# Feed-forward: both halves of a wide product's bank added in one VectorE operation of 512 columns

## The chip, the cores and the metric

One core of a Trainium2 chip runs the whole kernel. The metric is the device time of one execution in microseconds (us), the median over several runs; lower is better.

## The reference, cut to what matters

A trunk of two layers on a 512 x 1024 activation in float32: a pooling mixer in the first layer, chunked attention in the second, and after each a gated feed-forward block, which is what the change touches:

```python
def conv_ffn(h, w_gate, w_val, conv_w, conv_b, w_out):
    """out = (silu(causal_dwconv3(h W_gate)) * (h W_val)) W_out"""
    S = h.shape[1]
    a = h @ w_gate
    ap = jnp.pad(a, ((0, 0), (CONV_W - 1, 0), (0, 0)))
    a = ap[:, 0:S] * conv_w[0] + ap[:, 1:S + 1] * conv_w[1] + ap[:, 2:S + 2] * conv_w[2] + conv_b
    return (jax.nn.silu(a) * (h @ w_val)) @ w_out
# D_MODEL = 1024, SEQ = 512, D_FF = 2816, DEPTH = 2
x = x + conv_ffn(rmsnorm(x, ffn_norm[i]), ffn_w_gate[i], ffn_w_val[i], ffn_conv_w[i], ffn_conv_b[i], ffn_w_out[i])
```

## The kernel before

Activations lie with channels on the 128 partitions and the 512 frames along the columns. The hidden width of 2816 is cut into 22 blocks of 128, numbered f. Float32 precision comes from splitting each operand into a high part and a low part in a reduced format; a product is then high x high + high x low + low x high. ScalarE (ACT) makes the high part with a copy, VectorE (DVE) the low part with a subtraction (line 98 and line 99, in `split`).

Blocks 5 to 21 use Strassen's scheme (Winograd's form): gate and value of one block together take seven products of half the size (256 frames) instead of eight, and VectorE combines them. In blocks 8 to 21, `f in WIDE`, a product is "wide": one matmul of 512 columns multiplies the high part of the weights by the high and the low part of the activations side by side, so that the results land in the two halves of one PSUM bank, `o[:, 0]` and `o[:, 1]`; a matmul of 256 columns adds the low part of the weights into the first half. A wide product is therefore finished only when the two halves of its bank have been added. With 14 wide blocks in each of two layers there are 28.

A wide block f runs through these steps, one per `yield` of `strassen`:

1. product b11 into bank m; ACT copies both halves into the tile `a`
2. product b21 into a bank of its own, b (`side`)
3. product t2 on top of b11 in bank m; ACT copies both halves into the tile `val` (v in the profile)
4. product t3 into bank t (again `side`)
5. product t1 on top in bank m; the result, and t3 from bank t, go to the second half of `val`
6. product b22 on top in bank m, which makes the second half of `a`
7. product t4 on top of t3 in bank t, which makes the first half of `val`; then `hidden` does the convolution on `a`, the activation, the multiplication by `val` and the split of the result into the slot of block f

So b22 cannot start before ACT has copied t1 out of bank m, and t4 cannot start before VectorE has read t3 out of bank t. The weights of the products are split as g1 (from the gate weights), g2 (from the sum tile sa), g3 (from sb) and g4 (second half of the value weights); all four bear the names g_f_h and g_f_l. The sums sa and sb are VectorE additions of the raw weights gv. The high part of g3 sits in a tile with a single buffer, so ACT can write g3 of block f only after b22 of block f-1 has read its own.

Steps 6 and 7 of a block run between the first steps of the next one, and matmuls of the output product of the group of blocks before (`out`, on weights ow, added into X) are put in between. PE's sequence is written out by hand this way (`manual_schedule`); the sequences of ACT and VectorE are made by a list scheduler from priorities and its own cost estimates, so an edit of one instruction can move others. `tc.high_priority()` raises the priority of what it encloses. Scratch tiles of 512 columns come from tag g with six buffers.

Of the kernel before, what the change touches and what calls it, by code (L numbers as in the profile page):

```python
# [19 lines left out]
AF = mybir.ActivationFunctionType  # L20
# [20 lines left out]
HALF = S // 2  # L41
# [27 lines left out]
def trunk(ctx: ExitStack, tc: tile.TileContext, xt, xT, cols, band, edge, poolw, gv, wout, wqk, wv, wo, rel, out):  # L69
    nc = tc.nc  # L70
# [14 lines left out]
    def psum(tag, name, bufs=2):  # L85
        return ps.tile([P, S], F32, name=name, tag=tag, bufs=bufs)
# [3 lines left out]
    def g_tile(name):  # L90
        return tmp.tile([P, S], F32, name=name, tag="g", bufs=6)

    def split(raw, hi, lo, eng=None, eng_hi=None):

        if eng_hi:
            eng_hi.tensor_copy(hi, raw)
        else:
            nc.scalar.activation(hi, raw, AF.Copy)  # L98
        return (eng or nc.vector).tensor_sub(lo, raw, hi.bitcast(F32))  # L99
# [17 lines left out]
    def mm3(o, sh, sl, mh, ml, first, last, **how):  # L117

        yield nc.tensor.matmul(o, sh, mh, start=first, stop=False, **how)  # L119
        yield nc.tensor.matmul(o, sh, ml, start=False, stop=False, **how)  # L120
        yield nc.tensor.matmul(o, sl, mh, start=False, stop=last, **how)  # L121

    def run(steps):
        step = None
        for step in steps:
            pass
        return step
# [249 lines left out]
    def ffn(l, first, pool, acc, summed=None):  # L377
# [7 lines left out]
        def raw_tile(name, src, n=1024, own=False):  # L385
            raw = pool.tile([P, GM * P], F32, name=f"{name}_r", tag="or") if own else wp.tile([P, 1024], F32, name=f"{name}_r", tag="wr")
            nc.sync.dma_start(raw[:, :n], src)
            return raw
# [4 lines left out]
        def sum_tile(name):  # L393
            return pool.tile([P, 1024], F32R, name=name, tag="as", bufs=2).bitcast(F32)

        def parts(raw, n, name, out_=False, later=False):

            if out_:
                hi, lo = (out_tile(f"{name}_{c}", c) for c in "hl")
            elif next(ring) == "w":  # L400
                hi, lo = (wp.tile([P, 1024], F32R, name=f"{name}_{c}", tag=f"w{c}", bufs=2) for c in "hl")
            else:
                hi, lo = (pool.tile([P, 1024], F32R, name=f"{name}_{c}", tag=f"b{c}", bufs=1) for c in "hl")
            if later:
                nc.scalar.activation(hi[:, :n], raw[:, :n], AF.Copy)
                return hi, lo, lambda: nc.vector.tensor_sub(lo[:, :n], raw[:, :n], hi[:, :n].bitcast(F32))
            split(raw[:, :n], hi[:, :n], lo[:, :n])
            return hi, lo
# [4 lines left out]
        def hidden(f, a, finish):  # L413

            cw = [col[:, C_CW[l] + 4 * f + j:C_CW[l] + 4 * f + j + 1] for j in range(4)]
            c = g_tile(f"c{f}")
            nc.scalar.activation(c, a, AF.Identity, scale=cw[2], bias=cw[3])  # L417
            for j in range(1, 3):
                nc.vector.scalar_tensor_tensor(c[:, j:], a[:, :S - j], cw[2 - j], c[:, j:], op0=OP.mult, op1=OP.add)  # L419
            silu = nc.scalar.activation(c, c, AF.Silu)  # L420
            if l == 0 and f == NF - 1:
                with tc.issue_after(silu.ins):
                    nc.scalar.preload_act_table_set("natural_log_exp_and_others")
            finish(c)
            split(c, *slot[f])
# [152 lines left out]
        def strassen(f):  # L578

            g, v = (raw_tile(f"gv{l}_{f}_{i}", gv[l, f, i]) for i in range(2))  # L580
            sa, sb = (sum_tile(f"s{x}{f}") for x in "ab")
            a11, a12, a21, a22, s2, s3, s1, s4 = (x[:, z * S:(z + 1) * S] for x in (g, v, sa, sb) for z in range(2))
            nc.vector.tensor_add(s1, a21, a22)
            nc.vector.tensor_sub(s2, s1, a11)
            nc.vector.tensor_sub(s3, a11, a21)
            nc.vector.tensor_sub(s4, a12, s2)
            wide = f in WIDE

            def bank(tag, name):
                return psum(tag, f"st{l}_{f}_{name}", 4 if tag == "S" else 2).rearrange("p (c n) -> p c n", c=2)  # L590

            def product(o, hl, z, name, first):


                hi, lo = hl
                cs = [slice((4 * z + i) * P, (4 * z + i + 1) * P) for i in range(4)]
                how = {"skip_group_check": not first}
                if not wide:
                    for i, c in enumerate(cs):
                        run(mm3(o[:, 0], hi[:, c], lo[:, c], B[i, name][:, 0], B[i, name][:, 1], first and i == 0, i == 3, **how))  # L600
                    return
                for i, c in enumerate(cs):
                    nc.tensor.matmul(o, hi[:, c], B[i, name], start=first and i == 0, stop=False, **how)  # L603
                for i, c in enumerate(cs):
                    nc.tensor.matmul(o[:, 0], lo[:, c], B[i, name][:, 0], start=False, stop=i == 3, **how)  # L605

            def add(x, o):
                for c in range(2 if wide else 1):
                    nc.vector.tensor_add(x, x, o[:, c])  # L609

            def copy(x, rest=None):

                if wide and rest is None:
                    nc.scalar.activation(x, main.rearrange("p c n -> p (c n)"), AF.Copy)
                    nc.vector.tensor_add(x[:, :HALF], x[:, :HALF], x[:, HALF:])
                else:
                    x = x[:, HALF:] if rest is not None else x[:, :HALF]
                    nc.scalar.activation(x, main[:, 0], AF.Copy)  # L618
                    if wide:
                        if rest is not main:  # L620
                            nc.scalar.activation(rest, main[:, 1], AF.Copy)  # L621
                        nc.vector.tensor_add(x, x, main[:, 1] if rest is main else rest)

            a = pool.tile([P, S], F32, name=f"a{f}", tag="a", bufs=2)
            main, side = bank("S", "m"), bank("P", "b")
            w = parts(g, 1024, f"g1_{f}")
            product(main, w, 0, "b11", True)
            copy(a)
            yield
            product(side, w, 1, "b21", True)  # L630
            add(a[:, :HALF], side)
            yield
            val = g_tile(f"v{f}")
            w = parts(sa, 1024, f"g2_{f}")
            product(main, w, 0, "t2", False)
            copy(val)
            yield
            side = bank("S", "t")
            product(side, w, 1, "t3", True)
            yield  # L640
            w = parts(sb, 1024, f"g3_{f}")
            last = [tmp.tile([P, S], F32R, name=f"g4_{f}_{c}", tag="g", bufs=6) for c in "hl"]
            split(a22, *last)
            product(main, w, 0, "t1", False)
            with tc.high_priority():
                copy(val, a[:, HALF:])
                add(val[:, HALF:], side)
            yield
            product(main, w, 1, "b22", False)
            copy(a, main)  # L650
            yield
            product(side, last, 0, "t4", False)
            add(val[:, :HALF], side)
            hidden(f, a, lambda c: nc.vector.tensor_mul(c, val, c))
            yield

# [15 lines left out]
        with tc.manual_schedule(engines={mybir.EngineType.PE}):  # L672
            h, seed, known, made = early()
            queue, left, n = [], 0, 0
# [309 lines left out]
    with tc.tile_pool(name="ba", bufs=1) as big:  # L984
        rest = attention()
# [55 lines left out]
```

## Time and profile before

| | |
|---|---|
| median of 3 runs | 976.81 us (975.59 to 977.13) |
| the profiled execution | 976.21 us |
| its span, first to last instruction | 974.4 us |
| busy: PE matmul / weight load | 964.4 / 818.9 us |
| busy: VectorE / ScalarE / GpSimd | 810.5 / 578.8 / 103.2 us |
| mean granted TensorE clock | 0.999 |

A timeline row reads: start in us from the span's start, duration in us, engine, line, operation, out<-in by the program's names, shapes, count, and in brackets the idle time of the engine before it with what ended it. PEld is TensorE's weight load, which overlaps the matmuls. In the profile, names leave out buffer and block numbers: `st_m`, `st_b` and `st_t` are the banks m, b and t, v is `val`, c is the tile in which `hidden` works, out is a bank of the output product, `one`, u0h and the like are slots of finished hidden blocks. Instructions of one engine overlap: the next starts a little before the one before has ended.

### The profile page before, as it was taken

Reading aid. Unit: us, or ns where it says so; the run is one execution under the profiler, and the core shown is the slowest. Engines: PE = TensorE matmul, PEld = TensorE weight load, DVE = VectorE, ACT = ScalarE, POOL = GpSimd, SP = SyncE. Lnnn points to the kernel's source line nnn. Section 1 sums busy time; section 2 is a strip of 40 time slices with the busy share of each in tenths; the row PEclk is TensorE's granted clock in tenths of the full one; section 3 lists DMA queues with packets and bytes.
Section 4 is the critical chain, followed back from the end, with each engine's and each line's share of the span. In section 5 each row is a group of like instructions: output and inputs, shape, how many; then the busy total and the mean of one; then the engine's idle time right before and its main releaser. Section 6 shows DMA issues by size and latency. Waiting matters only on the chain.

```text
span 974.4 us, 14095 instructions
## 1 busy us (share of the span) xinstructions
PE 964.4 (99%) x5038; PEld 818.9 (84%) x5038; DVE 810.5 (83%) x1508; ACT 578.8 (59%) x1018; POOL 103.2 (11%) x90
## 2 busy tenths in 40 slices
PE   9999999999999999999999999999999999999998
PEld 8788988888888888888888787888998888888886
DVE  8999989999999854442777888999999999999953
ACT  7665565555556444344898988646555555555521
POOL 2300000000000013203534532000000000000000
PEclk9999999999999999999999999999999999999999
DMA  8222233232332234232343341332323323233223
GB/s 341 72 96 92 92 114 112 81 126 91 114 111 70 71 84 150 87 117 99 109 117 108 96 118 54 100 108 79 114 92 121 114 90 119 86 109 119 73 61 112
DMA packets 37430, 102.85 MB, mean 106 GB/s; under 512 B 4432, under 2 KB 7904, under 8 KB 37360
## 3 DMA queue, kind: packets, MB, share of 16 engines
q1 hardware_dynamic: 37296, 101.90, 33.1%
q8 instruction: 40, 0.66, 0.3%
q14 instruction: 30, 0.25, 0.1%
q0 software_dynamic: 32, 0.04, 0.0%
q10 hardware_dynamic: 32, 0.00, 0.0%
HBM read 95.60 MB, written 2.14 MB: 100 GB/s over the span
## 4 chain that ended last, share of the span: by engine, by line
PE 85%; DVE 10%; ACT 2%; DMA 1%; issue 1%; DVEq 0%; ACTq 0%
PE st_m L603 9%; PE out L119 8%; PE out L120 8%; PE out L121 8%; PE st_t L603 5%; PE st_m L605 5%; PE gv L120 3%; PE qk L120 3%; PE qk L119 3%; PE qk L121 3%; PE gv L119 3%; PE gv L121 3%; PE st_t L605 2%; PE st_b L603 2%; DVE g_l L99 2%; PE tp L872 2%
## 5 line engine op out<-in xcount | busy, mean ns | idle before, releaser
L120 PE MATMUL out<-one,ow_h 128*128 128x512 f32 x224 | 87.9, 392 | 0.0
L119 PE MATMUL out<-one,ow_h 128*128 128x512 f32 x224 | 87.8, 392 | 0.0
L121 PE MATMUL out<-one,ow_l 128*128 128x512 f32 x224 | 87.8, 392 | 0.0
L98 ACT ACTIVATE ow_h<-wo_r 128x640 fp32r<-128x640 f32 (+1 forms) x64 | 50.5, 789 | 55.3 <-PE out L120 46.2
L668 DVE TENSOR_TENSOR X<-out,X 128x512 f32<-128x512 f32 (+1 forms) x65 | 43.9, 677 | 35.9 <-PE out L121 35.9
L603 PE MATMUL st_m<-two,g_h 128*128 128x512 f32 x224 | 70.0, 394 | 0.2
L603 PE MATMUL st_m<-h,g_h 128*128 128x512 f32 x224 | 69.0, 389 | 0.0
L98 ACT ACTIVATE g_h<-gv_r 128x512 fp32r<-128x512 f32 (+1 forms) x68 | 57.3, 842 | 17.7 <-PE st_b L603 12.3
L99 DVE TENSOR_TENSOR g_l<-gv_r,g_h 128x512 fp32r<-128x512 f32 (+1 forms) x68 | 64.5, 949 | 0.2
L99 DVE TENSOR_TENSOR ow_l<-wo_r,ow_h 128x640 fp32r<-128x640 f32 (+1 forms) x64 | 56.4, 882 | 2.5 <-ACT ow_h L98 2.5
L419 DVE SCALAR_TENSOR_TENSOR c<-a,col,c 128x511 f32<-128x511 f32 (+1 forms) x76 | 56.2, 742 | 1.8 <-ACT c L417 1.8
L121 PE MATMUL qk<-wqk_h,two 128*128 128x512 f32 x128 | 51.4, 402 | 0.0
L119 PE MATMUL qk<-wqk_h,two 128*128 128x512 f32 x128 | 50.9, 409 | 0.0
L120 PE MATMUL qk<-wqk_l,two 128*128 128x512 f32 x128 | 50.8, 397 | 0.0
L609 DVE TENSOR_TENSOR v<-v,st_t 128x256 f32<-128x256 f32 x120 | 49.4, 412 | 1.0 <-ACT v L618 0.6
L603 PEld LDWEIGHTS st_m<-two,g_h 128*128 128x128 f32 x224 | 41.6, 188 | 10.3 <-ACT a L621 1.1
L603 PEld LDWEIGHTS st_m<-h,g_h 128*128 128x128 f32 x224 | 42.1, 188 | 9.6
L605 PEld LDWEIGHTS st_m<-two,g_l 128*128 128x128 f32 x224 | 42.0, 188 | 8.8
L98 ACT ACTIVATE g_h<-sb 128x1024 fp32r<-128x1024 f32 x34 | 36.0, 1059 | 20.2 <-PE st_m L603 17.5
L121 PEld LDWEIGHTS out<-one,ow_l 128*128 128x128 f32 x224 | 42.3, 189 | 6.4
L119 PEld LDWEIGHTS out<-one,ow_h 128*128 128x128 f32 x224 | 42.3, 189 | 6.1
L120 PEld LDWEIGHTS out<-one,ow_h 128*128 128x128 f32 x224 | 42.4, 189 | 5.3
(365 smaller groups left out, 2925.3 us busy)
## 6 DMA issues: line engine op xcount, KB each, us to landing
gv_r<-gv SPq DMA_DIRECT2D x86, 512.0 KB, 3.6
wo_r<-wout SPq DMA_DIRECT2D x32, 384.0 KB, 3.4
wo_r<-wout SPq DMA_DIRECT2D x32, 320.0 KB, 2.9
wqk_r<-wqk SPq DMA_DIRECT2D x16, 512.0 KB, 3.4
wv_r<-wv SPq DMA_DIRECT2D x8, 512.0 KB, 3.4
wo_r<-wo SPq DMA_DIRECT2D x8, 512.0 KB, 3.5
xt<-xt SPq DMA_DIRECT2D x4, 512.0 KB, 5.5
X<-xT SPq DMA_DIRECT2D x8, 256.0 KB, 7.3
```

The source lines that it names most:

```text
L98: nc.scalar.activation(hi, raw, AF.Copy)
L99: return (eng or nc.vector).tensor_sub(lo, raw, hi.bitcast(F32))
L119: yield nc.tensor.matmul(o, sh, mh, start=first, stop=False, **how)
L120: yield nc.tensor.matmul(o, sh, ml, start=False, stop=False, **how)
L121: yield nc.tensor.matmul(o, sl, mh, start=False, stop=last, **how)
L419: nc.vector.scalar_tensor_tensor(c[:, j:], a[:, :S - j], cw[2 - j], c[:, j:], op0=OP.mult, op1=OP.add)
L603: nc.tensor.matmul(o, hi[:, c], B[i, name], start=first and i == 0, stop=False, **how)
L605: nc.tensor.matmul(o[:, 0], lo[:, c], B[i, name][:, 0], start=False, stop=i == 3, **how)
L609: nc.vector.tensor_add(x, x, o[:, c])
L668: nc.vector.tensor_add(X[d][:, fs], o[:, fs], X[d][:, fs])
L872: nc.tensor.transpose(tp[:, j * P:(j + 1) * P], s_[:, j * P:(j + 1) * P], ident)
```

## The change

For a wide block the change adds both halves of a bank to a tile of 512 columns in one VectorE operation, and folds the two halves of that tile together afterwards (`fold`), where before each half of the bank was added to 256 columns on its own. This is done for b21 into `a` and for t3 into a new scratch tile `both_` (w in the profile, from tag g). ACT copies t1 with one operation of 512 columns into `both_`, where it made two copies of 256, into `val` and into the second half of `a`. For b22 and t4 the additions stay as they were. In the code of b11 the fold moves behind the addition of b21. Per wide block VectorE then has two additions of 512 columns and six of 256 instead of ten of 256, and ACT one copy of 512 instead of two of 256.

```diff
-            def add(x, o):
-                for c in range(2 if wide else 1):
-                    nc.vector.tensor_add(x, x, o[:, c])
-            def copy(x, rest=None):
...
+            def flat(o):
+                return o.rearrange("p c n -> p (c n)")
+            def fold(out, x):
+                nc.vector.tensor_add(out, x[:, :HALF], x[:, HALF:])
...
             product(main, w, 0, "b11", True)
-            copy(a)
+            if wide:
+                nc.scalar.activation(a, flat(main), AF.Copy)
...
             product(side, w, 1, "b21", True)
-            add(a[:, :HALF], side)
+            if wide:
+                nc.vector.tensor_add(a, a, flat(side))
+                fold(a[:, :HALF], a)
...
             product(main, w, 0, "t2", False)
-            copy(val)
+            if wide:
+                nc.scalar.activation(val, flat(main), AF.Copy)
+                fold(val[:, :HALF], val)
...
             product(main, w, 0, "t1", False)
             with tc.high_priority():
-                copy(val, a[:, HALF:])
-                add(val[:, HALF:], side)
+                if wide:
+                    both_ = g_tile(f"w{f}")
+                    nc.scalar.activation(both_, flat(main), AF.Copy)
+                    nc.vector.tensor_add(both_, both_, flat(side))
...
+            if wide:
+                fold(val[:, HALF:], both_)
             yield
             product(main, w, 1, "b22", False)
-            copy(a, main)
+            nc.scalar.activation(a[:, HALF:], main[:, 0], AF.Copy)
+            if wide:
+                nc.vector.tensor_add(a[:, HALF:], a[:, HALF:], main[:, 1])
             yield
             product(side, last, 0, "t4", False)
-            add(val[:, :HALF], side)
+            for c in range(2 if wide else 1):
+                nc.vector.tensor_add(val[:, :HALF], val[:, :HALF], side[:, c])
```

PE's sequence stays the same instruction for instruction. VectorE and ScalarE get new ones. Three places follow, in rows of line, operation, out<-in, shape; the long numbers in the names only tell buffers apart and differ between the two kernels.

VectorE in the first layer, from the first combination of t1 and t3 of block 10 (v_1715 is its `val`, a_1640 its `a`; a_1786 is `a` of block 11), before:

```order
L622 TENSOR_TENSOR v_1715<-v_1715,a_1640 128x256
L654 TENSOR_TENSOR c_1704<-v_1577,c_1704 128x512
L615 TENSOR_TENSOR a_1786<-a_1786 128x256
L583 TENSOR_TENSOR sb_1914<-gv_12_1_r 128x512
L609 TENSOR_TENSOR v_1715<-v_1715,st_10_t 128x256
L99 TENSOR_TENSOR g_11_l<-sb_1781,g_11_h 128x1024
L622 TENSOR_TENSOR a_1640<-a_1640,st_10_m 128x256
L99 TENSOR_TENSOR one_94<-c_1704,one_86 128x512
L609 TENSOR_TENSOR v_1715<-v_1715,st_10_t 128x256
L609 TENSOR_TENSOR a_1786<-a_1786,st_11_b 128x256
```

and now:

```order
L649 TENSOR_TENSOR w_1755<-w_1755,st_10_t 128x512
L664 TENSOR_TENSOR c_1699<-v_1574,c_1699 128x512
L583 TENSOR_TENSOR sb_1906<-gv_12_1_r 128x512
L611 TENSOR_TENSOR v_1710<-w_1755 128x256
L99 TENSOR_TENSOR g_11_l<-sb_1775,g_11_h 128x1024
L659 TENSOR_TENSOR a_1636<-a_1636,st_10_m 128x256
L99 TENSOR_TENSOR one_94<-c_1699,one_86 128x512
L624 TENSOR_TENSOR a_1780<-a_1780,st_11_b 128x512
```

The last reading of bank t of block 10 (st_10_t) moved from the ninth row to the first.

ScalarE in the first layer, around the copy of t1 of block 11 (c_1842 and c_1835 are the tile of `hidden` of block 10), before:

```order
L98 ACTIVATE g_12_h<-sa_1913 128x1024
L420 ACTIVATE c_1842<-c_1842 128x512
L618 ACTIVATE v_1854<-st_11_m 128x256
L621 ACTIVATE a_1786<-st_11_m 128x256
L614 ACTIVATE a_1919<-st_12_m 128x512
L98 ACTIVATE one_87<-c_1842 128x512
L98 ACTIVATE g_12_h<-sb_1914 128x1024
```

and now:

```order
L98 ACTIVATE g_12_h<-sa_1905 128x1024
L648 ACTIVATE w_1887<-st_11_m 128x512
L98 ACTIVATE g_12_h<-sb_1906 128x1024
L420 ACTIVATE c_1835<-c_1835 128x512
L618 ACTIVATE a_1911<-st_12_m 128x512
L657 ACTIVATE a_1780<-st_11_m 128x256
```

The split of g3 of block 12 (g_12_h<-sb) moved ahead of the activation of hidden tile 10; the second layer has the same. VectorE's `g_12_l<-sb` moved in the same way, ahead of the multiplication c<-v,c of tile 10.

ScalarE in the first layer, around the copy of t1 of block 12 (c_1977 and c_1968 are the tile of `hidden` of block 11, u0h the high part of its result), before:

```order
L98 ACTIVATE g_13_h<-sa_2056 128x1024
L618 ACTIVATE v_1989<-st_12_m 128x256
L621 ACTIVATE a_1919<-st_12_m 128x256
L420 ACTIVATE c_1977<-c_1977 128x512
L614 ACTIVATE a_2062<-st_13_m 128x512
L98 ACTIVATE u0h<-c_1977 128x512
```

and now:

```order
L420 ACTIVATE c_1968<-c_1968 128x512
L98 ACTIVATE g_13_h<-sa_2046 128x1024
L98 ACTIVATE u0h<-c_1968 128x512
L648 ACTIVATE w_2035<-st_12_m 128x512
L618 ACTIVATE a_2052<-st_13_m 128x512
```

The copy of bank m moved behind the activation and u0h of block 11. In the second layer it stands between the two, ahead of u0h.

More of the change, by code (lines that the diff above doesn't have):

```diff
@@ L605, in product @@
                     nc.tensor.matmul(o[:, 0], lo[:, c], B[i, name][:, 0], start=False, stop=i == 3, **how)
-            def add(x, o):
-                for c in range(2 if wide else 1):
-                    nc.vector.tensor_add(x, x, o[:, c])
-            def copy(x, rest=None):
[L613 to L622, printed above, removed]
+            def flat(o):
+                return o.rearrange("p c n -> p (c n)")
+            def fold(out, x):
+                nc.vector.tensor_add(out, x[:, :HALF], x[:, HALF:])
             a = pool.tile([P, S], F32, name=f"a{f}", tag="a", bufs=2)
@@ L627, in strassen @@
             product(main, w, 0, "b11", True)
-            copy(a)
+            if wide:
+                nc.scalar.activation(a, flat(main), AF.Copy)
+            else:
+                nc.scalar.activation(a[:, :HALF], main[:, 0], AF.Copy)
             yield
             product(side, w, 1, "b21", True)
-            add(a[:, :HALF], side)
+            if wide:
+                nc.vector.tensor_add(a, a, flat(side))
+                fold(a[:, :HALF], a)
+            else:
+                nc.vector.tensor_add(a[:, :HALF], a[:, :HALF], side[:, 0])
             yield
@@ L635, in strassen @@
             product(main, w, 0, "t2", False)
-            copy(val)
+            if wide:
+                nc.scalar.activation(val, flat(main), AF.Copy)
+                fold(val[:, :HALF], val)
+            else:
+                nc.scalar.activation(val[:, :HALF], main[:, 0], AF.Copy)
             yield
@@ L645, in strassen @@
             with tc.high_priority():
-                copy(val, a[:, HALF:])
-                add(val[:, HALF:], side)
+                if wide:
+                    both_ = g_tile(f"w{f}")
+                    nc.scalar.activation(both_, flat(main), AF.Copy)
+                    nc.vector.tensor_add(both_, both_, flat(side))
+                else:
+                    nc.scalar.activation(val[:, HALF:], main[:, 0], AF.Copy)
+                    nc.vector.tensor_add(val[:, HALF:], val[:, HALF:], side[:, 0])
+            if wide:
+                fold(val[:, HALF:], both_)
             yield
             product(main, w, 1, "b22", False)
-            copy(a, main)
+            nc.scalar.activation(a[:, HALF:], main[:, 0], AF.Copy)
+            if wide:
+                nc.vector.tensor_add(a[:, HALF:], a[:, HALF:], main[:, 1])
             yield
             product(side, last, 0, "t4", False)
-            add(val[:, :HALF], side)
+            for c in range(2 if wide else 1):
+                nc.vector.tensor_add(val[:, :HALF], val[:, :HALF], side[:, c])
             hidden(f, a, lambda c: nc.vector.tensor_mul(c, val, c))
```

## The prediction

> **What bounds the kernel.** I read the page first: the engines' busy time and the chain that ended last.
>
> ```profile
> span 974.4 us, 14095 instructions
> PE 964.4 (99%) x5038; PEld 818.9 (84%) x5038; DVE 810.5 (83%) x1508; ACT 578.8 (59%) x1018; POOL 103.2 (11%) x90
> ```
>
> TensorE (PE) is busy 99% of the span, and the change touches no matmul: PE executes the same instructions in the same sequence. So only time in which PE stands still can be won. The wide blocks (f = 8 to 21) run from about 125 to 336 us in the first layer and from about 719 to 930 us in the second. The list of PE's waits and of its weight loads' (PEld's) waits from 170 to 340 us, and then from 764 to 934 us, is complete in these rows (us in total, times, longest):
>
> ```profile
> PE st_t L603 <- DVE v L609: 1.0, 1, 1.0
> PEld st_t L603 <- DVE v L609: 1.9, 2, 1.4
> PEld st_m L603 <- ACT a L621: 0.5, 1, 0.5
> ...
> PE st_t L603 <- DVE v L609: 0.5, 1, 0.5
> PEld st_t L603 <- DVE v L609: 1.8, 3, 0.9
> PEld st_m L603 <- ACT a L621: 0.5, 1, 0.5
> ```
>
> Two causes only. `st_t <- DVE v L609`: product t4 writes into the bank that t3 filled, and has to wait until VectorE (DVE) has read t3 out. `st_m <- ACT a L621`: product b22 writes into bank m, and waits for ScalarE's (ACT's) copy of t1. What PE loses is smaller than PEld's idle time, so I take it from PE's timeline (start, duration): the distance of starts less the usual one.
>
> ```profile
> 174.31 0.40 PE L120 MATMUL out<-u3l,ow_h 128*128 128x512 f32 x1
> 174.55 0.39 PE L121 MATMUL out<-u3h,ow_l 128*128 128x512 f32 x1
> 175.90 0.50 PE L603 MATMUL st_t<-two,g_h 128*128 128x512 f32 x1 [0.96 <-DVE v L609]
> ...
> 280.62 0.39 PE L120 MATMUL out<-u3l,ow_h 128*128 128x512 f32 x1
> 281.09 0.73 PE L603 MATMUL st_t<-two,g_h 128*128 128x512 f32 x2
> ...
> 768.29 0.39 PE L121 MATMUL out<-u3h,ow_l 128*128 128x512 f32 x1
> 769.19 0.73 PE L603 MATMUL st_t<-two,g_h 128*128 128x512 f32 x2 [0.51 <-DVE v L609]
> ...
> 873.90 0.39 PE L120 MATMUL out<-u3l,ow_h 128*128 128x512 f32 x1
> 874.38 0.74 PE L603 MATMUL st_t<-two,g_h 128*128 128x512 f32 x2
> ...
> 332.68 0.39 PE L121 MATMUL out<-u3h,ow_l 128*128 128x512 f32 x1
> 333.18 0.50 PE L603 MATMUL st_m<-two,g_h 128*128 128x512 f32 x1
> ```
>
> A 512-column matmul follows the one before after 174.55 - 174.31 = 0.24 us. So t4 lost 1.35 - 0.24 = 1.11 (f = 10), 0.47 - 0.24 = 0.23 (f = 17), 0.90 - 0.24 = 0.66 and 0.48 - 0.24 = 0.24 us in the second layer: 2.24 us together. The fifth t4 wait shows with PEld alone (three times there, two of them above) and may have cost PE 0.1 us. b22 of f = 21 lost 0.50 - 0.24 = 0.26 us in each layer. All that the wide blocks can give is 2.24 + 0.1 + 0.52, some 2.9 us.
>
> **The change, part by part.**
>
> *VectorE's instructions.* Per wide block and layer, ten additions of 256 columns become six of 256 and two of 512. This is VectorE's timeline ahead of the longest stall:
>
> ```profile
> 170.57 0.41 DVE L622 TENSOR_TENSOR v<-v,a 128x256 f32<-128x256 f32 x1
> 170.90 0.68 DVE L654 TENSOR_TENSOR c<-v,c 128x512 f32<-128x512 f32 x1
> ...
> 173.03 0.42 DVE L609 TENSOR_TENSOR v<-v,st_t 128x256 f32<-128x256 f32 x1
> 173.36 1.22 DVE L99 TENSOR_TENSOR g_l<-sb,g_h 128x1024 fp32r<-128x1024 f32 x1
> 174.50 0.42 DVE L622 TENSOR_TENSOR a<-a,st_m 128x256 f32<-128x256 f32 x1
> 174.83 0.69 DVE L99 TENSOR_TENSOR one<-c,one 128x512 fp32r<-128x512 f32 x1
> 175.43 0.41 DVE L609 TENSOR_TENSOR v<-v,st_t 128x256 f32<-128x256 f32 x1
> 175.76 0.41 DVE L609 TENSOR_TENSOR a<-a,st_b 128x256 f32<-128x256 f32 x1
> ```
>
> From start to start an addition takes 0.33 us at 256 columns (175.43 to 175.76, from PSUM; 170.57 to 170.90, from SBUF) and 0.60 at 512 (174.83 to 175.43). Ten become 6 x 0.33 + 2 x 0.60 = 3.18 instead of 3.30 us, 28 times: 3.4 us less VectorE work. None of it is on PE's path, since PE waited for VectorE only at the five places above; I count it as nothing. [...]
>
> *t3's bank.* Before, its two readers stood apart: the first at 173.03, the second at 175.43, behind three other instructions; PE resumed at 175.90, 0.06 us after the second ended. Afterwards one 512-column addition stands where `v<-v,a` stood (170.57), and the bank is free at about 171.3, over 3 us before PE asks for it at 174.78. In the other wide blocks, too, the one reader stands where the first of two stood, or ahead of it. I count all four measured waits as gone and the fifth too: -2.24 - 0.1 = -2.3 us. What is late next is b22's bank m, at f = 12 by 200.86 - 198.71 = 2.15 us (rows below).
>
> *ScalarE's copies.* Two copies of 256 become one of 512:
>
> ```profile
> 179.70 0.60 ACT L614 ACTIVATE v<-st_m 128x512 f32<-128x512 f32 x1 [0.76 <-PE st_m L605]
> ...
> 183.33 0.39 ACT L618 ACTIVATE v<-st_m 128x256 f32<-128x256 f32 x1
> 183.61 0.38 ACT L621 ACTIVATE a<-st_m 128x256 f32<-128x256 f32 x1
> ...
> 186.43 1.06 ACT L98 ACTIVATE g_h<-sb 128x1024 fp32r<-128x1024 f32 x1 [0.19 <-PE st_m L603]
> ```
>
> 183.33 to 183.99 was 0.66, now 0.60: m is free 0.06 us sooner, which PE feels at f = 21 alone: -0.1 us over both layers.
>
> *Moved instructions.* The scheduler built a new sequence around f = 11 and 12. ScalarE now splits g3 of block 12 (`g_h<-sb`, the row at 186.43) ahead of the activation of hidden tile 10, and VectorE takes the matching `g_l<-sb` ahead of that tile's c<-v,c. This split must wait for PE (the row's releaser), so both engines stand until 186.43 and then have everything else behind them. In the first layer alone, the copy of t1 of f = 12, on which b22 waits, stands behind `u0h<-c`, and that behind VectorE's c<-v,c of tile 11. From 187.49 (end of `g_h`) to the end of that c<-v,c VectorE has 21 instructions: two of 1024 columns, one of 768, ten of 512, two of 510, six of 256. The remaining rows needed:
>
> ```profile
> 198.33 0.38 ACT L621 ACTIVATE a<-st_m 128x256 f32<-128x256 f32 x1
> ...
> 197.97 0.74 DVE L419 SCALAR_TENSOR_TENSOR c<-a,col,c 128x510 f32<-128x510 f32 x1
> 198.63 1.21 DVE L99 TENSOR_TENSOR g_l<-sa,g_h 128x1024 fp32r<-128x1024 f32 x1
> ...
> 200.11 0.68 DVE L654 TENSOR_TENSOR c<-v,c 128x512 f32<-128x512 f32 x1
> ...
> 200.82 0.63 ACT L98 ACTIVATE u0h<-c 128x512 fp32r<-128x512 f32 x1
> ...
> 200.86 0.62 PE L603 MATMUL st_m<-two,g_h 128*128 128x512 f32 x2
> ```
>
> 2 x 1.14 (173.36 to 174.50) + 0.87 (midway between 0.60 and 1.14) + 9 x 0.60 + 2 x 0.66 (197.97 to 198.63) + 6 x 0.33 + 0.68 (the last, to its end) = 12.5. So c ends at 187.5 + 12.5 = 200.0, u0h starts at once and hands on after 0.55 (0.63 less the overlap of 0.08), the copy ends at 200.0 + 0.55 + 0.60 = 201.2; PE wants m at 200.86 (the last row). Both ends of this sum ride on PE, so it holds even if PE comes 1.1 us earlier, as long as VectorE reaches the gate in time; before, it had more work ahead of `g_l<-sb` than now. New wait: 201.2 + 0.05 - 200.86 = 0.4 us. It may be nothing, if the 21 take 3% less. At the other end, a weight tile's landing falls into the stretch: VectorE's waits from 170 to 340 us and from 764 to 934 us have
>
> ```profile
> DVE sb L583 <- DMA gv_r<-gv: 5.9, 8, 1.1
> ...
> DVE sb L583 <- DMA gv_r<-gv: 5.6, 7, 1.4
> ```
>
> so up to 1.1 us more. I take 0.4, since here the load is issued 1 us earlier than before and its user stands later. In the second layer the copy stands ahead of u0h, behind an activation whose input comes five instructions and 3.0 us earlier in the same sum: no wait. The other positions that changed (the activation ahead of the copy at f = 13, 14; loads for the output products against gate weights in SyncE's queue) leave over a microsecond by the same kind of sum; I count nothing.
>
> *Another scratch tile per block* in the six slots of tag g adds one wait of ScalarE on its own earlier write; nothing.
>
> **Sum.** -2.3 - 0.1 + 0.4 = -2.0 us. The profiled execution took 976.21 us (span 974.4 and 1.8 around it), 0.6 below the median of the runs, 976.81. The sum gives 974.2 for an execution like the profiled one and 974.8 against the median, which I predict. A difference of 0.2%, 1.95 us, is about what a measurement can tell from no change; the forecast lies on that edge.
>
> **The rivals.**
>
> A, the forecast: the t4 waits go, block 12 of the first layer waits 0.1 to 1.5 us: 974.5 to 975.9, likeliest 974.8. Chance 0.50.
>
> B, no new wait: -2.4, 974.4. For it: 0.4 us is 3% of a 12.5 us sum. Against it: VectorE has little air there, and a landing only adds. The row of the stretches from 175 to 340 us (length; busy time of PE, PEld, DVE, ACT, POOL):
>
> ```profile
> 175.00:340.00 165.00, 163.90 (x857) 139.74 (x858) 153.57 (x267) 92.32 (x143) 0.00 (x0) 1.00 0.31 95
> ```
>
> 153.57 of 165 is 93%. Chance 0.17.
>
> C, the gain is given back: VectorE meets a landing in the long stretch in both layers, and b22 of block 12 waits 1.2 us in each: 2.4 us, 976.8. For it: the DMA rows above, and the gate stands in both layers. Against it: in the second layer the copy is not behind u0h. 0.25.
>
> D, slower, by the gate at block 12: ScalarE and VectorE stand at the split of g3 in both layers and hand the delay on, so that b22 waits 2.7 us in each: 5.4 - 2.4 = 3.0 us more, 979.8. It decides from 2.4 + 1.95 = 4.4 us of new waits. For it: nothing behind the gate can pass it. Against it: the sum leaves 0.4 us, and another 2.3 would take two of the longest landings each time. 0.08.
>
> **Numbers.** Half of A (0.25), B (0.17) and little more lie below 974.86: faster 0.44; same 0.48; slower 0.08. Range 973.9 (all 2.9 us) to 977.1 (C, and the highest run before, 977.13).
>
> **What would show it.** The profile after should have no wait `st_t <- DVE` in the wide blocks, the 512-column addition of w ending over 2 us ahead of t4; two 512-column additions at about 0.68 us each; the b22 wait of f = 21 at about 0.2 us; and a new wait of PE on ScalarE's copy of w at about 200 us in the first layer, none near 794 us in the second. Wrong I would be if PE's waits of the wide blocks sum to over 2 us, or if PE waits for a weight part g_l, for which it waited nowhere here.

## The result, and the profile after

The kernel after takes 977.26 us, the median of 22 runs (976.97 to 980.62), against 976.36 us for 22 runs of the kernel before (975.36 to 977.85). The ratio is 1.0014, with a 95% interval of 1.0008 to 1.0021: about 0.1% slower, where the forecast was 0.2% faster. The profiled execution took 977.40 us, 1.2 us more than that of before. The first lines of its page:

```profile
span 975.6 us, 13968 instructions
PE 962.5 (99%) x5038; PEld 817.7 (84%) x5038; DVE 806.1 (83%) x1452; ACT 575.5 (59%) x990; POOL 103.2 (11%) x90
```

VectorE has 1508 - 1452 = 56 instructions and 4.4 us of work less. Yet the span is 1.2 us longer. The list of PE's and PEld's waits in the kernel after, from 170 to 340 us and then from 764 to 934 us (us in total, times, longest):

```profile
PE out L120 <- DVE one L99: 1.9, 1, 1.9
PEld out L120 <- DVE one L99: 2.3, 1, 2.3
PEld st_m L603 <- ACT w L648: 0.4, 1, 0.4
...
PE out L120 <- DVE one L99: 1.9, 1, 1.9
PEld out L120 <- DVE one L99: 2.3, 1, 2.3
PEld st_m L603 <- ACT w L648: 0.4, 1, 0.4
```

Every `st_t <- DVE` row of before is gone, as forecast. In their place stands one wait per layer that no row of before has: the output product waits for VectorE to finish the low part of a hidden tile (`one`). PE's timeline of the kernel after shows its size:

```profile
190.36 0.40 PE L119 MATMUL out<-one,ow_h 128*128 128x512 f32 x1
192.61 0.50 PE L120 MATMUL out<-one,ow_h 128*128 128x512 f32 x1 [1.85 <-DVE one L99]
...
784.39 0.40 PE L119 MATMUL out<-one,ow_h 128*128 128x512 f32 x1
786.64 0.50 PE L120 MATMUL out<-one,ow_h 128*128 128x512 f32 x1 [1.85 <-DVE one L99]
```

The starts are 2.25 us apart instead of 0.23: 2.02 us lost in each layer. The matmul reads hidden tile 10, the last of the group of blocks 5 to 10. ScalarE's timeline of the kernel after, from the copy of t1 of block 11, and VectorE's up to that tile's low part:

```profile
181.56 0.60 ACT L648 ACTIVATE w<-st_m 128x512 f32<-128x512 f32 x1 [0.80 <-PE st_m L605]
185.43 1.06 ACT L98 ACTIVATE g_h<-sb 128x1024 fp32r<-128x1024 f32 x1 [3.27 <-PE st_m L603]
186.40 0.61 ACT L420 ACTIVATE c<-c 128x512 f32<-128x512 f32 x1
...
188.60 0.63 ACT L98 ACTIVATE one<-c 128x512 fp32r<-128x512 f32 x1
```

```profile
186.52 1.23 DVE L99 TENSOR_TENSOR g_l<-sb,g_h 128x1024 fp32r<-128x1024 f32 x1 [1.30 <-ACT g_h L98]
187.66 0.69 DVE L664 TENSOR_TENSOR c<-v,c 128x512 f32<-128x512 f32 x1
188.27 0.42 DVE L611 TENSOR_TENSOR v<-w 128x256 f32<-128x256 f32 x1
188.60 0.42 DVE L659 TENSOR_TENSOR a<-a,st_m 128x256 f32<-128x256 f32 x1
188.93 0.68 DVE L624 TENSOR_TENSOR a<-a,st_b 128x512 f32<-128x512 f32 x1
189.53 0.69 DVE L583 TENSOR_TENSOR sb<-gv_r 128x512 f32<-128x512 f32 x1
190.13 0.69 DVE L585 TENSOR_TENSOR sa<-gv_r,gv_r 128x512 f32<-128x512 f32 x1
190.73 1.22 DVE L99 TENSOR_TENSOR g_l<-gv_r,g_h 128x1024 fp32r<-128x1024 f32 x1
191.87 0.69 DVE L99 TENSOR_TENSOR one<-c,one 128x512 fp32r<-128x512 f32 x1
```

This is the gate that the prediction described. ScalarE stands 3.27 us until PE has finished b22 of block 11 (from 183.49 on it could have run the activation of tile 10, whose last input VectorE had finished by then), VectorE 1.30 us until ScalarE has written the high part of g3 of block 12; the activation of tile 10 and its multiplication c<-v,c come after that, and the tile's low part eight instructions behind the gate. It ends at 192.56, and PE goes on at 192.61. In the kernel before, VectorE's timeline has the same two operations the other way round:

```profile
186.50 0.68 DVE L99 TENSOR_TENSOR one<-c,one 128x512 fp32r<-128x512 f32 x1
...
189.17 1.22 DVE L99 TENSOR_TENSOR g_l<-sb,g_h 128x1024 fp32r<-128x1024 f32 x1
```

There the low part of tile 10 ended at 187.18, and the product that reads it ran at its usual distances (starts at 191.37, 191.60 and 191.83).

The balance over the wide blocks, by the starts of the same matmuls in both kernels: the stretch from 125.08 to 340.21 us before lies at 125.33 to 340.81 after, and that from 720.09 to 930.09 at 720.62 to 931.32. That is 0.35 and 0.70 us longer, 1.05 together. The two new waits are +4.04, so about 3.0 us went. The single distances say where: the four t4 waits (2.3), b22 of f = 21 (0.24), and 0.11 us more behind each t4 wait, where the matmul that follows comes late, too. PE's timeline of the kernel before shows this behind the longest one:

```profile
175.90 0.73 PE L603 MATMUL st_t<-two,g_h 128*128 128x512 f32 x2 [0.96 <-DVE v L609]
176.47 0.62 PE L603 MATMUL st_t<-h,g_h 128*128 128x512 f32 x2
```

The two rows start 0.57 us apart, elsewhere 0.46 (335.38 and 335.84).

### The profile page after: what moved, and what is told of

Same layout as the page of the kernel before. It is cut to its first block, busy times and chain, and to the rows that moved or that the text cites. A ratio compares the mean times of both kernels' runs of the same rounds, so it can differ in the third digit from the quotient of the medians.

```text
span 975.6 us, 13968 instructions
## 1 busy us (share of the span) xinstructions
PE 962.5 (99%) x5038; PEld 817.7 (84%) x5038; DVE 806.1 (83%) x1452; ACT 575.5 (59%) x990; POOL 103.2 (11%) x90
## 4 chain that ended last, share of the span: by engine, by line
PE 90%; DVE 7%; ACT 2%; issue 1%; DMA 1%; SPq 0%; DVEq 0%; ACTq 0%
PE st_m L603 11%; PE out L120 8%; PE out L121 8%; PE out L119 8%; PE st_m L605 5%; PE st_t L603 5%; PE gv L120 3%; PE qk L120 3%; PE qk L119 3%; PE qk L121 3%; PE gv L121 3%; PE gv L119 3%; PE st_t L605 3%; PE st_b L603 2%; PE tp L882 2%; PE oo L894 2%
## 5 line engine op out<-in xcount | busy, mean ns | idle before, releaser
L99 DVE TENSOR_TENSOR g_l<-sb,g_h 128x1024 fp32r<-128x1024 f32 x34 | 41.6, 1223 | 10.4 <-ACT g_h L98 10.4
```

## The experiments

The theory: the time is lost because hidden tile 10 stands behind the split of g3 of block 12 on ScalarE and VectorE, and the output product needs its low part. The rivals: the gate itself costs time whoever waits behind it; the new instructions of VectorE do; or it is the new order elsewhere. PE's instructions stand in the same order in all seven kernels that follow.

**1. The gate moved back (`pin12`).** The split of g3 of block 12 is queued behind the split of tile 10 on both engines (`split2` does what `split` does, and returns its two instructions):

```diff
-            split(c, *slot[f])
+            done[f] = split2(c, *slot[f])
...
-            w = parts(sb, 1024, f"g3_{f}")
+            with ExitStack() as behind:
+                if f == 12:
+                    for x in done[f - 2]:
+                        behind.enter_context(tc.issue_after(x.ins))
+                w = parts(sb, 1024, f"g3_{f}")
```

> The changed kernel, with the split of g3 of block 12 queued behind the split of hidden tile 10, on ScalarE and on VectorE. Theory (the loss is one wait per layer of the output product on hidden tile 10, whose split stands behind the gate at g3 of block 12): that wait of 2.0 us goes in both layers, no t4 wait comes back, and what is left of PE's waits in the wide blocks is b22 of f = 21, 0.15 us by start distances in each layer; against the kernel before -2.24 - 0.1 - 0.2 = -2.5 us, ratio 0.9974, about 973.9 us. Rival (the 512-column additions hold VectorE up, and the output product only happened to be the one that felt it): a wait of 1 to 2 us per layer shows up at another product, ratio 0.9995 to 1.002.

Measured: 973.55 us (973.53 to 973.92), ratio 0.9969 [0.9957, 0.9980]. With one split pinned, and what the scheduler rearranged behind it, 3.7 us went: more than the change had lost, so that this kernel is faster than both. In `pin12`, VectorE's timeline in the first layer has the low part of tile 10 ahead of the gate's again:

```profile
188.74 0.69 DVE L102 TENSOR_TENSOR one<-c,one 128x512 fp32r<-128x512 f32 x1
189.34 0.42 DVE L614 TENSOR_TENSOR a<-a 128x256 f32<-128x256 f32 x1
189.68 1.22 DVE L99 TENSOR_TENSOR g_l<-sb,g_h 128x1024 fp32r<-128x1024 f32 x1
```

Of PE's waits for tile 10 one is left, in the second layer: `out <- DVE one`, 0.3 us in the list, 0.48 by the distance of starts.

**2. The gate put into the kernel before (`gate_before`).** The kernel before with its 256-column additions; only the activation and the multiplication of tile 10 are queued behind the split of g3 of block 12 (`w[2]` holds that split's two instructions):

```diff
+            done[f] = [silu]
...
-            hidden(f, a, lambda c: nc.vector.tensor_mul(c, val, c))
+            hidden(f, a, lambda c: done[f].append(nc.vector.tensor_mul(c, val, c)))
...
-            w = parts(sb, 1024, f"g3_{f}")
+            w = parts(sb, 1024, f"g3_{f}", both=True)
+            if f == 12:
+                for late_, early_ in zip(done[f - 2], w[2]):
+                    tc.add_manual_dep(late_.ins, early_.ins.name, mybir.DependencyInfo(mybir.DependencyClass.NoSync, mybir.DependencyReason.DATA), reason="gate")
```

> The kernel before, with all its 256-column additions, but the activation of hidden tile 10 queued behind the split of g3 of block 12 on ScalarE, and that tile's multiplication behind the low part of the split on VectorE. Theory: the sequence alone makes the loss. By the durations of the profile before, VectorE ends the low part of hidden tile 10 at 187.5 + 5.8 = 193.3 us, and the output product asks for it at 191.6: a wait of about 1.7 us in each layer, on top of the waits of before; +3.4 us, ratio 1.0035, about 979.8. Rival (the 512-column additions are at fault): no such wait, ratio within 0.1% of 1.

Measured: 984.56 us (983.54 to 988.38), ratio 1.0085 [1.0071, 1.0098]. The direction is the theory's: with none of the new instructions, the gate alone makes the kernel slower, so the loss doesn't need the 512-column additions. The size is not: 8 us instead of 3.4. The wait at the output product is 3.03 us per layer by the starts, where a sum of raw weights now stood ahead of the gate's low part on VectorE and waited for its load:

```profile
188.37 0.69 DVE L589 TENSOR_TENSOR sb<-gv_r 128x512 f32<-128x512 f32 x1 [1.75 <-DMA gv_r<-gv]
188.99 1.22 DVE L102 TENSOR_TENSOR g_l<-sb,g_h 128x1024 fp32r<-128x1024 f32 x1
...
194.06 0.68 DVE L99 TENSOR_TENSOR one<-c,one 128x512 fp32r<-128x512 f32 x1
```

The rest of the 8 us lies in a slower stretch of matmuls behind the wait of the second layer (granted clock 0.50 from 792 to 794 us; last section) and in t4 waits that grew by 0.6 us in all.

**3. That landing taken out of the way (`gate_before2`).** As 2, and the first sum `sb` of block 13 is queued behind the gate's low part on VectorE, too.

```diff
-            nc.vector.tensor_add(s1, a21, a22)
+            first_ = nc.vector.tensor_add(s1, a21, a22)
+            if f == 13:
+                tc.add_manual_dep(first_.ins, done["gate"].ins.name, mybir.DependencyInfo(mybir.DependencyClass.NoSync, mybir.DependencyReason.DATA), reason="gate")
```

> As gate_before (the kernel before with the activation, multiplication and split of hidden tile 10 queued behind the split of g3 of block 12), and the first sum sb of block 13 queued behind that split on VectorE as well, so that no landing of a weight tile stands ahead of the gate's low part. Theory (gate_before lost more than the kernel after because VectorE waited 1.75 us for a landing ahead of the low part): the wait before the output product falls from 3.03 to about 1.7 us per layer, and the time from 984.56 by 2.7 us to about 981.9, 1.0057. Rival (the landing only moved a wait that was due anyway, or the loss lies elsewhere): the wait stays at about 3 us and the time at 984.5, 1.0085.

Measured: 984.43 us (982.70 to 986.16), ratio 1.0083 [1.0069, 1.0096]. By the time this is the rival's result. The trace says why. The gate's low part came 1.92 us earlier (187.07 instead of 188.99), but the wait fell only by 0.68, from 3.03 to 2.35 us per layer by the starts, not to 1.7. Two things that the expectation doesn't name took the rest in the first layer. The sum `sb`, queued behind the gate, now stands ahead of `one`: from the start of the gate's low part to that of `one` (192.75) it is 5.68 us instead of 194.06 - 188.99 = 5.07. And PE came to the product 0.62 us earlier (the matmul ahead of the wait starts at 190.91 instead of 191.53). On top there is a cost that neither side had listed, and that stands in the trace of `gate_before`, too. Rows of stretches of this kernel (length; busy time of PE, PEld, DVE, ACT, POOL; granted TensorE clock, DMA share, GB/s), behind the wait in the first layer and behind that in the second:

```profile
193.00:196.00 3.00, 2.51 (x13) 2.14 (x14) 3.00 (x7) 1.17 (x2) 0.00 (x0) 1.00 0.00 0
...
787.00:790.00 3.00, 0.82 (x4) 0.41 (x3) 3.00 (x6) 0.00 (x0) 0.00 (x0) 0.99 0.00 0
790.00:793.00 3.00, 3.00 (x11) 2.53 (x10) 3.00 (x6) 1.47 (x2) 0.00 (x0) 0.50 0.32 79
793.00:796.00 3.00, 3.00 (x16) 2.51 (x15) 2.71 (x6) 2.81 (x4) 0.00 (x0) 0.94 0.70 221
```

After PE's pause in the second layer the granted clock is 0.50 for 3 us. This kernel's four runs have a mean granted clock of 0.996 to 0.998, and the profiled one, with one such phase, is the fastest of them at 982.70 us; the profiled one of `gate_before`, with one phase as well, took 984.86. So experiment 3 shows a part of the wait going with the landing, and the medians don't settle how much time that is worth.

**4. Half of the change: b21 alone (`only_b21`).** `a` gets its 512-column addition and the late fold; t1 and t3 are handled as before.

```diff
-                    both_ = g_tile(f"w{f}")
-                    nc.scalar.activation(both_, flat(main), AF.Copy)
-                    nc.vector.tensor_add(both_, both_, flat(side))
...
-                fold(val[:, HALF:], both_)
+                    nc.scalar.activation(a[:, HALF:], main[:, 1], AF.Copy)
+                    nc.vector.tensor_add(val[:, HALF:], val[:, HALF:], a[:, HALF:])
+                for c in range(2 if wide else 1):
+                    nc.vector.tensor_add(val[:, HALF:], val[:, HALF:], side[:, c])
```

> Half of the change: the addition of b21 in one operation of 512 columns and its fold; t1, t3 as before. The second reading of t3 of block 10 stands where it stood before, seven rows behind the first. Theory: the t4 waits of block 10 stay (about 1.1 us in the first layer, 0.7 in the second), no wait on hidden tile 10, since its split is the third VectorE instruction behind the gate: ratio 0.9995 to 1.0005, 975.9 to 976.9 us. Rival (the 512-column addition costs time itself): half of the loss or more, ratio 1.0005 to 1.002.

Measured: 979.79 us (978.52 to 982.24), ratio 1.0033 [1.0022, 1.0043], a miss. The t4 waits were expected to stay as they were, and they grew. PE's waits of this kernel in the second layer, and VectorE's timeline around the two readings of t3 of block 18:

```profile
PE st_t L603 <- DVE v L651: 3.3, 2, 2.3
```

```profile
888.99 0.69 DVE L583 TENSOR_TENSOR sb<-gv_r 128x512 f32<-128x512 f32 x1 [1.85 <-DMA gv_r<-gv]
889.59 0.41 DVE L651 TENSOR_TENSOR v<-v,st_t 128x256 f32<-128x256 f32 x1
889.92 1.22 DVE L99 TENSOR_TENSOR g_l<-sb,g_h 128x1024 fp32r<-128x1024 f32 x1
891.06 0.41 DVE L656 TENSOR_TENSOR a<-a,st_m 128x256 f32<-128x256 f32 x1
891.39 0.68 DVE L99 TENSOR_TENSOR one<-c,one 128x512 fp32r<-128x512 f32 x1
891.99 0.41 DVE L651 TENSOR_TENSOR v<-v,st_t 128x256 f32<-128x256 f32 x1
```

VectorE waits 1.85 us for a landing ahead of the first reading, where the kernel before waited 0.70, and then three instructions stand between the two readings, where there was one: bank t of block 18 is free 2.4 us too late. What the t3 half removes can also grow; it depends on what the scheduler puts ahead of the two readings and between them.

**5. The other half: t1 and t3 alone (`only_t3`).** One copy of t1, one 512-column addition of t3 and the fold; b21 with two additions as before, and b11 folded at once.

```diff
-                nc.vector.tensor_add(a, a, flat(side))
-                fold(a[:, :HALF], a)
+                for c in range(2):
+                    nc.vector.tensor_add(a[:, :HALF], a[:, :HALF], side[:, c])
```

> The other half: t1 copied in one operation of 512 columns, t3 added in one of 512 and folded; b21 as before. ScalarE's activation of hidden tile 10 stands ahead of the gate, but VectorE's low part of that tile still stands behind it, after the split of g1 of block 13. Theory: no t4 wait; the low part ends at 187.5 + 0.3 + 0.6 + 0.7 + 1.1 + 0.7 = 190.9 us and is asked for at 190.6, a wait of 0.1 to 0.5 us per layer: -2.4 + 0.6 = -1.8 us, ratio 0.998, about 974.6 us. Rival (512-column additions at fault): between before and the changed kernel, ratio 1.000 to 1.001.

Measured: 974.09 us (973.40 to 974.42), ratio 0.9973 [0.9962, 0.9984], as expected. This half alone comes close to `pin12`. With it the scheduler leaves the activation and the multiplication of tile 10 ahead of the gate. The split of the tile still stands behind it, but nearer. VectorE's timeline of `only_t3`:

```profile
186.09 1.23 DVE L99 TENSOR_TENSOR g_l<-sb,g_h 128x1024 fp32r<-128x1024 f32 x1
...
189.64 0.68 DVE L99 TENSOR_TENSOR one<-c,one 128x512 fp32r<-128x512 f32 x1
```

From start to start it is 3.55 us instead of 5.35, and the output product waits 0.2 and 0.5 us by the starts. In `only_b21` the low part of tile 10 starts 1.74 us behind that of the gate, and the product doesn't wait for it. So the slow order at block 12 belongs to neither half alone: it came when both were put together.

**6. The reader taken away, the gate left (`slot`).** The kernel after; the output product's first block of channels reads the slot of block 9 in place of block 10, so that block 10's share of these channels is left out of the result.

```diff
-   *slot[b + i]
+   *slot[b + i - (g == 1 and d == 0 and i == 5)]
```

> The kernel after, but the output product's matmuls for block 10 of the first 128 channels read the finished slot of block 9; block 10's share of these channels is left out of the result. The gate at block 12 stays where it is. Theory (the time is lost because this product reads hidden tile 10, queued behind the gate): PE's wait before it, 2.02 us in each layer, goes, and little comes in its place, since the next reader of tile 10 stands 2 us later: 977.3 - 4.0, some 973.3 us, 0.9965 of the kernel before; ScalarE still stands about 3 us at the gate. Rival (the gate itself costs time, or VectorE's new instructions do): the wait moves to the next thing behind the gate, the copy of t1 of block 12 or the first reader of tile 10 in the next output product; 975.5 to 977.3 us, 0.9990 to 1.0008.

Measured: 972.86 us (972.72 to 973.26), ratio 0.9965 [0.9952, 0.9978]. ScalarE's timeline of `slot` at the gate, and the whole list of PE's and PEld's waits from 170 to 340 us, which is the same from 764 to 934:

```profile
185.40 1.06 ACT L98 ACTIVATE g_h<-sb 128x1024 fp32r<-128x1024 f32 x1 [3.27 <-PE st_m L603]
```

```profile
PEld st_m L603 <- ACT w L648: 0.4, 1, 0.4
```

The gate stands unchanged, with the same 3.27 us of ScalarE's idle time, and costs PE nothing. What cost 4 us was one reader behind it. One thing this run can't show: further on the scheduler's order changed, too, and the copy of t1 of block 12 starts at 197.08 us, ahead of u0h at 202.91. So the small wait that the prediction saw at this copy was not put to the test.

**7. The last wait (`pin13`).** As `pin12`; in the second layer the split of g1 of block 13, too, is queued behind the split of tile 10.

```diff
-            w = parts(g, 1024, f"g1_{f}")
+            with ExitStack() as behind:
+                if l == 1 and f == 13:
+                    for x in done[10]:
+                        behind.enter_context(tc.issue_after(x.ins))
+                w = parts(g, 1024, f"g1_{f}")
```

> As pin12, and in the second layer the split of g1 of block 13 is queued behind the split of hidden tile 10 too, since there its low part stood 1.14 us ahead of that tile's low part and the output product waited 0.48 us. Theory: that wait goes, no other comes; 973.1 us, 0.9964, with PE's waits in the wide blocks down to the two of b22 at block 21 (0.22 us each). Rival: b11 of block 13 or the sums behind it come late in turn; 973.5 us or more, 0.9969 or above.

Measured: 972.99 us (972.85 to 973.18), ratio 0.9966 [0.9953, 0.9978]. The list of waits from 764 to 934 us now has one row, and it is the same in the first layer:

```profile
PEld st_m L606 <- ACT w L659: 0.5, 1, 0.5
```

Against `pin12` the gain, 0.6 us, is within what separate comparisons can tell (the intervals overlap); the trace shows that the 0.48 us wait is gone and none came. This is the version to keep: the change with two orders pinned, 0.34% faster than before.

## Why the prediction was wrong, point by point

- *The t4 waits go: right.* None is left, and the 512-column addition of w takes 0.68 us; that of block 10 ends at 170.98, 4 us before t4 starts at 175.03.
- *What they are worth: too small.* By the starts of the same matmuls the two stretches take 425.13 us before and 422.06 in `pin13`: 3.1 us gained, though b22 of f = 21 still waits there, against 2.4 for the forecast without a new wait and 2.9 as the most that the wide blocks could give. The sum took each t4 wait by the distance ahead of its first matmul and left out the 0.11 us behind it, about half a microsecond in all.
- *ScalarE's one copy: right in kind.* b22 of f = 21 lost 0.15 instead of 0.26 us, 0.2 us over both layers against 0.1.
- *The gate at block 12: seen, and followed to the wrong reader.* This is the step that failed. The prediction counted 21 instructions of VectorE from the gate's low part on and asked only who waits for the last, c<-v,c of tile 11. The ninth of them, tile 10's low part, has a reader too: the output product. Its wait stands in no term of the sum, which counts nothing for the other positions, and it measured 4.04 us where the sum had 0.4 for the gate. The same sum would have given it: 1.14 + 0.60 + 2 x 0.33 + 3 x 0.60 + 1.14 = 5.34 us from the gate's low part to the start of `one`, and the trace has 5.35. PE's timeline of the kernel before has the reader:

```profile
191.60 0.39 PE L120 MATMUL out<-one,ow_h 128*128 128x512 f32 x1
```

  With the gate's high part ending at 187.49 there, `one` would have run from some 192.8 to 193.5, 1.9 us behind its reader. Measured: 2.02.
- *The 0.4 us at the copy of t1 of block 12: the length of the stretch was right, the wait didn't come.* ScalarE's and PE's timelines of the kernel after:

```profile
199.12 0.63 ACT L98 ACTIVATE u0h<-c 128x512 fp32r<-128x512 f32 x1 [1.36 <-DVE c L664]
199.66 0.58 ACT L648 ACTIVATE w<-st_m 128x512 f32<-128x512 f32 x1
...
201.98 0.62 PE L603 MATMUL st_m<-two,g_h 128*128 128x512 f32 x2
```

  From the end of `g_h` (185.43 + 1.06) to the start of u0h it took 12.6 us, against 12.5 summed. The copy ended at 200.24. PE asked for the bank at 201.98; without the 2.02 us lost before, it would have asked at 199.96 and waited an estimated 0.3 us. So the other wait probably covered this one; that isn't shown, since in `pin12`, `only_t3` and `slot` the scheduler put the copy ahead of u0h.
- *Rivals.* The measured 977.26 lies nearest to C, "the gain is given back", 976.8, and just above the range's end of 977.1. But C's mechanism, a landing that VectorE meets, did not happen in that stretch of this kernel: VectorE's waits from 186 to 202 us and from 780 to 796 us have no DMA row. It shows in `gate_before` (1.75 us) and `only_b21` (1.85 us). Rival D named the right mechanism, the gate handing its delay on in both layers, and the wrong reader: b22 instead of the output product. Its argument against itself, that the sum left only 0.4 us, was made for that reader alone.
- *The signs of error.* The prediction named two: PE's waits of the wide blocks adding up to over 2 us, and PE waiting for a weight part g_l. The first came. What PE waited for was the low part of a hidden tile, not of the weights.

## What to carry to other kernels

When a change lets a scheduler put a waiting instruction further forward on an engine that, like ScalarE and VectorE here, lets nothing behind it pass (in the kernel after ScalarE stood 3.27 us and VectorE 1.30, each with an instruction behind the gate whose input was there: the activation of tile 10 from 183.49 on, v<-w from 185.22 on), list every instruction that now stands behind it and look up the reader of each, not only of the last; add the durations from the gate to each, and set them against the time at which the reader asks. An edit that removes waits can be worth keeping though the first build is slower: compare the waits of the two traces, and if a new one stands in a single place, pin that one order (here one split, 3.7 us). Halves of a change tell less than one would hope under a list scheduler, since each half gets an order of its own.

## What the runs showed of the hardware

In `gate_before2` and `gate_before` a pause of PE was followed by a slower stretch that cost more time. In `gate_before2` PE paused 2.18 us in each layer; in the second the granted clock then read 0.50 for some 3.4 us (an estimate from the 0.99, 0.50 and 0.94 of the rows under experiment 3), in the first 1.00. The matmuls' starts show it as well:

```profile
789.54 0.50 PE L123 MATMUL out<-one,ow_h 128*128 128x512 f32 x1 [2.18 <-DVE one L99]
...
790.25 1.05 PE L611 MATMUL st_m<-two,g_h 128*128 128x512 f32 x2
791.11 1.05 PE L611 MATMUL st_m<-h,g_h 128*128 128x512 f32 x2
...
794.22 0.62 PE L611 MATMUL st_t<-h,g_h 128*128 128x512 f32 x2
```

Two matmuls take 0.86 us from start to start (790.25 to 791.11) instead of 0.46 (794.22 to 794.68). From the matmul that waited to this `st_t<-h` it is 4.68 us (789.54 to 794.22), in the first layer 3.15 (193.49 to 196.64): the phase cost 1.5 us. `gate_before`, with 2.77 us, has the same picture: 0.50 in the second layer (792 to 794 us), 1.00 in the first (190 to 200 us). Not every pause was followed by it in the profiled executions: behind the 1.85 us of the kernel after the clock read 1.00 in both layers (193 to 200 and 787 to 796 us), and behind the 2.25 us ahead of t4 in `only_b21` two matmuls take 0.47 us from start to start (893.03 to 893.50). So of seven pauses in the wide blocks between 1.85 and 2.77 us two had such a phase behind them. No run here shows what decides it.

It would explain the spread of the kernel after. Of its 22 runs, 14 lie between 976.97 and 977.40 us at a mean granted clock of 0.999 or 1.0, and eight between 978.47 and 980.62 at 0.996 to 0.998. One phase takes an estimated 0.002 off the mean clock (half the clock for 3.4 of 977 us), so the slowest run, at 0.996 and 3.4 us above the median, would have had two. The four versions without a pause over 0.5 us in the wide blocks (`pin12`, `only_t3`, `slot`, `pin13`; 22 runs) have 0.999 or 1.0 throughout. None of those eight runs was profiled, so where their clock fell isn't shown. They are also why the ratio is 1.0014 while that of the medians is 977.26 / 976.36 = 1.0009.
